# A Delta-rule stage moved from an automatic order into one explicit plan of all queues, with keys and queries no longer transposed on TensorE

## The chip, the cores and the metric

The kernel runs on one core of one Trainium2 chip. A core has TensorE (PE, whose weight loads are shown apart as PEld), VectorE (DVE), ScalarE (ACT), GpSimd (POOL) and SyncE (SP, used here only to issue DMAs). The metric is the device time of one launch in microseconds; lower is better.

## The reference

One decoder layer on a sequence of 1024 tokens, width 1024, float32. One normalised input feeds one projection; its columns go to two groups of heads that work in parallel:

```
h    = rms_norm(x, norm1_w);  proj = h @ w_in
A:   differential attention, 4 heads, two 64-wide softmax maps each
B:   gated DeltaNet, 4 heads of 128:
     qkv  = silu(causal_conv4(proj[...]))            # keys, queries, values
     q, k = l2_norm(q), l2_norm(k)
     L    = strict_lower(beta * k k^T * decay)       # per chunk of tokens
     u, w = solve(I + L, [beta v, beta k exp(g)])    # unit lower triangular
     state loop over chunks: v_new = u - w S;  o = q S + (q k^T * decay) v_new
                             S = S * exp(g_last) + k_dec^T v_new
x = x + concat(A, B) @ w_out
x = x + square(relu(rms_norm(x, norm2_w) @ w_up)) @ w_down
```

The chunk of the delta rule is free to choose as long as the result is the same; the kernel uses chunks of 128 tokens, eight for each head.

## The kernel before

**Arithmetic.** Large products are made as three float32r products of high and low parts (`hH`, `hL` for the input; `wH`, `wL` for weights). A weight piece comes from DRAM into `wraw`, ScalarE rounds it into `wH`, VectorE makes the rest `wL` (L303, L304; L1048, L1050 in the later part). Small products are plain float32.

**Order of the stages.** The normalised input and a first projection (`ps_z`, gates and decay inputs) come first, then the Delta stage, then the projections of group A (`da_units`, `ps_qk` and `ps_v`) overlapped with the scan of group B, attention, the output projection and the MLP.

**The Delta stage.** Six weight units are projected in the order keys, queries, values (`dn_proj(1)`, `dn_proj(0)`, `dn_proj(2)`), each unit two heads, each head two halves of 512 tokens: 24 tiles `ps_dn` of 24 products each, on TensorE at L309 to L311. A tile has the head's 128 channels on the partitions and 512 tokens (four chunks) along the row. Each tile is copied to `cp` (L761), convolved (one ScalarE operation, L763, and three VectorE operations, L765, into `cy`) and put through SiLU (L769 and L858 for keys, L773 else).

- Keys: the tile is parked in DRAM (L785), TensorE transposes it in four 128x128 pieces into `ps_t` (L813) and makes its Gram matrices `ps_m` (L820). ScalarE squares `ps_t` and accumulates each key's squared length (L865). From it VectorE makes the key scale `bp` = beta / length (L867 to L871) and the matrix `lt` = Gram * `bp` * decay (L877), and weights the transposed keys by `kds` (L882) for the scan. The diagonal 32x32 blocks of `lt` go to DRAM (`fsx_d`, L881). The decay matrices `dtm` come from rows loaded by GpSimd's queue (L830), two ScalarE operations (L834, L835) and a mask multiplied by GpSimd (L836).
- Queries: parked, transposed (L813) for their lengths (L938), multiplied with the reloaded keys (L820), scaled with `bp` and decay (L944), parked again. Between the tiles run the 31 steps of the blocks' inversion on VectorE (`invert`, L846 and L848).
- Values: turned by VectorE's 32x32 block transposition (L953) and stored with 128-byte runs (L791).
- The second half of the inverse (`horner`, L901 to L923) assembles the 128x128 inverses from the inverted blocks: products `ps_p` (L907) and three products `ps_h` (L915) a head, for two heads at a time, with VectorE and ScalarE between. Its result is `W`.

All of this stage was ordered by the framework's own scheduler.

**The explicit plan.** From `da_units` on, the class `Interleave` writes out by hand the order of every engine. Streams (`flow.add(priority, generator)`) emit TensorE work, tasks (`flow.task`) emit the operations of ScalarE (S), VectorE (V), GpSimd (G) and the DMA queues (P for SP, G for GpSimd). Each `yield` names an engine and a cost in ns, a time, or a condition. The plan keeps a clock for each engine, takes what can start first, and of several that are ready the one with the lower priority number, those ready for over 800 ns ahead of the others:

```
x = min(((r > s - SLACK, y.prio, y) for t, y, r in found
         if t <= s and isinstance(y.want, tuple) and y.want[0] == eng), key=lambda f: f[:2])[2]
```

A TensorE stream holds a PSUM bank (`flow.hold`) until a task leaves it. On the chip each engine runs its queue strictly in the written order. What the scheduler still orders (the last of the inverse's second half) falls between the written instructions; the plan allowed for it by a surcharge on the first products (`INVERSES`), and it started some steps at fixed times (`SCAN_START`, `NORM_START`, `EXP_AT`).

**The scan.** For each chunk c: products with the parked keys and the state (L1096), a remainder on VectorE (L1071), the product with `W` (L1105), a ScalarE copy `sy` (L1075), the product with the weighted keys (L1116), the update of the state on VectorE (L1084); beside it the outputs (L1148, L1164).

Of the kernel before, what the change touches and what calls it, by code (L numbers as in the profile page):

```python
# [18 lines left out]
P = 128  # L19
# [12 lines left out]
NORM_START = 12000.0  # L32
INVERSES = 650.0
BEGIN = -8400.0
BEFORE = dict(P=BEGIN + 2000.0)
SCAN_START = 29000.0
AHEAD = 3
EXP_AT = 16000.0
# [163 lines left out]
def act(n, accum=False):  # L202
    return "S", 55.0 + 0.83 * n + (280.0 if accum else 0.0)
# [23 lines left out]
def tile_hymba_layer(  # L227
# [54 lines left out]
    cg_d = dram.tile([32, P], F32, name="cg_d")  # L282
    qk_d = [dram.tile([P, SEQ], F32, name=f"qk_d{i}") for i in range(2 * HEADS)]
# [42 lines left out]
    make_identity(nc, ident)  # L326
    neghalf = const.tile([P, 32], F32, name="neghalf")
    V.memset(neghalf, -0.5)
    poshalf = const.tile([P, 4], F32, name="poshalf")
    V.memset(poshalf, 0.5)  # L330
# [22 lines left out]
    pj = pctx.enter_context(tc.tile_pool(name="pj", bufs=2, space=PSUM))  # L353
    p1ctx = ctx.enter_context(ExitStack())
    ph = p1ctx.enter_context(tc.tile_pool(name="ph", bufs=2, space=PSUM, side="right"))
# [360 lines left out]
    ps = ph.tile([P, 512], F32, tag="ph", name="ps_r")  # L716
    T.transpose(ps[0:32, 0:P], cg[:, 0:32], ident)
    V.tensor_copy(cgr, ps[0:32, 0:P])
    G.dma_start(cg_d, cgr)
# [6 lines left out]

    s1ctx = ExitStack()
    sf = s1ctx.enter_context(tc.tile_pool(name="sf", bufs=1, reuse_waits="tile", side="right"))
    sa = s1ctx.enter_context(tc.tile_pool(name="sa", bufs=1, reuse_waits="tile", side="right"))

    fx = sf.tile([P, 1024], F32, name="fx")
    fg = sf.tile([P, 1024], F32, name="fg")
    ft = sf.tile([P, 256], F32, name="ft")
    G.memset(fg, 0.0)
    G.memset(fg[:, ::33], 1.0)

    def ta(name, bufs, dt=F32):
        return sa.tile([P, 512], dt, tag=name, name=name, bufs=bufs)

    ssq, ssk, rq, bp, kds, vsc = smalls + [sp.tile([P, 32], F32, name=n) for n in ("kds", "vsc")]  # L740
    rvs = ssk

    cps = [sa.tile([P, 1028], F32, name=f"cp{i}") for i in range(2)]
    for cp in cps:
        V.memset(cp[:, 0:3], 0.0)

    copies = {}

    def dn_proj(kind):
        for pr in range(2):  # L750
            with tc.issue_after(x_last.ins) if kind == 1 and pr == 0 else ExitStack():
                w = load_unit(w_units[4 + 2 * kind + pr], behind=copies[1, 0, 0].ins if kind == 1 and pr == 1 else None)
            for hl in range(2):
                h = 2 * pr + hl
                u = 4 * kind + h
                cp = cps[hl]
                for hf in range(2):
                    ps = pj.tile([P, 512], F32, tag="pj", name="ps_dn")
                    trn(ps, w, hl * P, hf)
                    b = 512 * hf  # L760
                    copies[kind, h, hf] = S.copy(cp[:, 3 + b:3 + b + 512], ps)  # L761
                    y = ta("cy", 2)
                    S.activation(y, cp[:, 3 + b:3 + b + 512], AF.Copy, scale=pv[:, 36 + u:37 + u])  # L763
                    for wi in (2, 1, 0):
                        V.scalar_tensor_tensor(y, cp[:, wi + b:wi + b + 512], pv[:, 12 * wi + u:12 * wi + u + 1],  # L765
                                               y, ALU.mult, ALU.add)
                    if kind == 1:
                        th = ta("cth", 2)
                        S.activation(th, y, AF.Tanh, scale=0.5)  # L769
                        yield h, hf, y, th  # L770
                    else:
                        o = ta("cth" if hf else "k2", 2)
                        S.activation(o, y, AF.Silu)  # L773
                        yield h, hf, o

    def skew(gen):
        prev = None
        for it in gen:
            if prev is not None:
                yield prev  # L780
            prev = it
        yield prev

    def park(h, hf, slot, src):
        nc.sync.dma_start(park_d[h, 4 * hf:4 * hf + 4, :, slot, :].rearrange("c p d -> p c d"), v4(src))  # L785

    def put_blocks(dst, src):

        for a in range(4):
            s = slice(32 * a, 32 * a + 32)  # L790
            nc.sync.dma_start(dst[:, s].rearrange("(b s) r -> s b r", s=32),  # L791
                              src[s].rearrange("s (b r) -> s b r", r=32))

    def get_blocks(dst, src):

        k = dst.shape[1] // P
        src = src.rearrange("(a s) (k b r) -> b s k a r", s=32, k=k, r=32)
        for b in range(4):
            nc.sync.dma_start(dst[32 * b:32 * b + 32].rearrange("s (k a r) -> s k a r", k=k, r=32), src[b])
# [10 lines left out]
    def transposed(src):  # L810
        ps = pt_.tile([P, 512], F32, tag="pt", name="ps_t")
        for c in range(4):
            T.transpose(ps[:, c * P:(c + 1) * P], src[:, c * P:(c + 1) * P], ident)  # L813
        return ps

    def gram(l, r):
        ps = pm.tile([P, 512], F32, tag="pm", name="ps_m")
        for c in range(4):
            cs = slice(c * P, (c + 1) * P)
            T.matmul(ps[:, cs], l[:, cs], r[:, cs], start=True, stop=True)  # L820
        return ps

    dts = {}

    def decay(h, hf):
        if not dts:
            dts.update({(a, b): sa.tile([P, 512], F32, name=f"dtm{a}{b}") for a in range(HEADS) for b in range(2)})
        row = ta("row", 2)
        i = cidx(h, 4 * hf)
        G.dma_start(row, cg_d[i:i + 4, :].rearrange("i t -> (i t)").partition_broadcast(P))  # L830
        dtm = dts[h, hf]
        for c in range(4):
            cs = slice(c * P, (c + 1) * P)
            S.activation(dtm[:, cs], row[:, cs], AF.Relu, bias=cg[:, i + c:i + c + 1], scale=-1.0)  # L834
        S.activation(dtm, dtm, AF.Exp, scale=-1.0)  # L835
        G.tensor_tensor(v4(dtm), v4(dtm), bc_mask(tri), ALU.mult)  # L836

    def invert():

        fxv = fx.rearrange("p (j i) -> p j i", i=32)  # L840
        fgv = fg.rearrange("p (r c) -> p r c", c=32)
        nc.sync.dma_start(fx, fsx_d)
        for j in range(31):
            m = 31 - j
            tv = ft[:, :m * (j + 1)].rearrange("p (m c) -> p m c", m=m)
# [3 lines left out]
            if j % 8 == 7:  # L849
                yield  # L850
        nc.sync.dma_start(fsg_d, fg)

    lt = {}
    for h, hf, y, th in skew(dn_proj(1)):
        with tc.issue_after(copies[1, 0, 0].ins):
            decay(h, hf)
        k2 = ta("k2", 2)
        V.scalar_tensor_tensor(k2, th, 1.0, y, ALU.add, ALU.mult)  # L858
        park(h, hf, 0, k2)
        ps = transposed(k2)  # L860
        psm = gram(k2, k2)
        kn = ta("kn", 2)
        for c in range(4):
            i = cidx(h, 4 * hf + c)
            S.activation(kn[:, c * P:(c + 1) * P], ps[:, c * P:(c + 1) * P], AF.Square, accum_out=ssk[:, i:i + 1])  # L865
        sk = sp.tile([P, 4], F32, tag="sk", name="sk", bufs=2)
        V.tensor_scalar(sk, cols4(ssk, h, hf), 4.0 * EPS, None, ALU.add)  # L867
        r2 = sp.tile([P, 4], F32, tag="r2", name="r2", bufs=2)
        V.reciprocal(r2, sk)
        V.tensor_tensor(cols4(bp, h, hf), r2, cols4(beta, h, hf), ALU.mult)  # L870
        V.tensor_tensor(cols4(kds, h, hf), cols4(bp, h, hf), cols4(ediff, h, hf), ALU.mult)  # L871
        L = sp.tile([P, 512], F32, tag="lw", name="lt", bufs=10)
        lt[h, hf] = L
        for c in range(4):
            i = cidx(h, 4 * hf + c)
            cs = slice(c * P, (c + 1) * P)
            V.scalar_tensor_tensor(L[:, cs], psm[:, cs], bp[:, i:i + 1], dts[h, hf][:, cs], ALU.mult, ALU.mult)  # L877
        for b in range(4):
            bs = slice(32 * b, 32 * b + 32)
            p0 = 32 * h + 8 * b + 4 * hf  # L880
            nc.sync.dma_start(fsx_d[p0:p0 + 4, :].rearrange("c (j i) -> j c i", i=32), v4(L[bs, :])[:, :, bs])  # L881
# [65 lines left out]
    for _ in inverse:  # L947
        pass
# [1522 lines left out]
```

## Time and profile before

| | us |
|---|---|
| median of 3 runs | 1204.82 (1204.08 to 1206.37) |
| the profiled execution's own time | 1206.17 |
| its span, first to last instruction | 1204.5 |
| PE busy | 1188.2 |
| DVE busy | 853.3 |
| ACT busy | 610.9 |
| POOL busy | 152.2 |

The profiled execution's own time is 1.67 us more than its span, and 1.35 us above the median of the runs. In the profile's rows "idle before" is an engine's idle time just before an instruction, and the name behind the arrow is what ended it. The rows of a timeline give start, duration, engine, line, operation, the tiles written and read, and the count. TensorE is pipelined: durations of neighbouring matmuls overlap, and the distance of the starts is what one costs.

### The profile page before, as it was taken

What the parts mean: (1) busy time and instruction counts of PE and PEld (TensorE: products, weight loads), DVE (VectorE), ACT (ScalarE), POOL (GpSimd) and SP (SyncE); (2) the same over time, 40 slices, a digit from 0 to 9 for tenths busy, and PEclk for the clock granted to TensorE, in tenths of its full rate; (3) what the DMA queues carried; (4) which work ended last, traced back from release to release, by engine and by line L of the source; (5) the groups of instructions that cost most, each with busy time, mean ns of one, the idle gap of its engine ahead of it and who ended that gap; (6) DMA issues with size and microseconds to landing.
All of it is one profiled execution on the core that took longest, in us unless ns stands there. A gap on an engine that the chain in (4) does not pass through costs nothing.

```text
span 1204.5 us, 17444 instructions
## 1 busy us (share of the span) xinstructions
PE 1188.2 (99%) x6168; PEld 993.6 (82%) x6168; DVE 853.3 (71%) x1652; ACT 610.9 (51%) x1194; POOL 152.2 (13%) x191
## 2 busy tenths in 40 slices
PE   9999999999999999999999999999999999999998
PEld 8978888888887787888788888888888888888887
DVE  6869898647767889886895665456669755786543
ACT  6557553434546665774664544445553333333330
POOL 2425120023322432011100000000000000000000
PEclk9999999999999999999999999999999999999999
DMA  9345654565655586223546544344489455422401
GB/s 350 107 145 139 191 155 98 124 202 159 199 159 171 147 209 188 58 45 106 175 125 242 184 148 134 133 171 175 159 287 384 183 210 199 139 84 104 140 35 70
DMA packets 164494, 193.67 MB, mean 161 GB/s; under 512 B 63288, under 2 KB 119608, under 8 KB 164408
## 3 DMA queue, kind: packets, MB, share of 16 engines
q1 hardware_dynamic: 160136, 180.85, 47.2%
q0 software_dynamic: 4128, 11.72, 2.9%
q8 instruction: 48, 0.79, 0.3%
q14 instruction: 38, 0.31, 0.1%
q10 hardware_dynamic: 144, 0.00, 0.0%
HBM read 131.53 MB, written 61.00 MB: 160 GB/s over the span
## 4 chain that ended last, share of the span: by engine, by line
PE 83%; DVE 6%; DMA 4%; ACT 3%; issue 2%; POOL 1%; SPq 0%; POOLq 0%; DVEq 0%; ACTq 0%
PE X L2044 5%; PE X L2043 5%; PE X L2042 5%; PE X L2370 4%; PE X L2368 4%; PE X L2369 4%; PE ps_op L1829 2%; PE Y L2043 2%; PE Y L2042 2%; PE Y L2044 2%; PE ps_op L1831 2%; PE ps_op L1830 2%; PE ps_dn L311 2%; PE ps_dn L309 2%; PE Y L2368 2%
## 5 line engine op out<-in xcount | busy, mean ns | idle before, releaser
L1921 ACT CAST hH<-ur 128x1024 fp32r<-128x1024 f32 x56 | 58.8, 1050 | 173.3 <-PE Y L2369 89.4
L1922 DVE TENSOR_TENSOR hL<-ur,hH 128x1024 fp32r<-128x1024 f32 x56 | 68.4, 1223 | 79.5 <-ACT hH L1921 79.3
L1922 DVE TENSOR_TENSOR op<-raw,op 128x1024 fp32r<-128x1024 f32 x48 | 58.7, 1223 | 73.7 <-PE X L2043 40.4
L2370 PE MATMUL X<-hH,hL 128*128 128x512 f32 x224 | 87.2, 389 | 0.0
L2369 PE MATMUL X<-hL,hH 128*128 128x512 f32 x224 | 87.2, 389 | 0.0
L2368 PE MATMUL X<-hH 128*128 128x512 f32 x224 | 87.2, 389 | 0.0
L309 PE MATMUL ps_dn<-hH,wH 128*128 128x512 f32 x192 | 76.1, 396 | 1.8 <-ACT cp L761 1.8
L310 PE MATMUL ps_dn<-hL,wH 128*128 128x512 f32 x192 | 75.6, 394 | 0.0
L311 PE MATMUL ps_dn<-hH,wL 128*128 128x512 f32 x192 | 75.4, 393 | 0.0
L1922 DVE TENSOR_TENSOR hL<-dw,hH 128x1024 fp32r<-128x1024 f32 x56 | 68.2, 1219 | 1.0 <-ACT hH L1921 1.0
L1921 ACT CAST op<-raw 128x1024 fp32r<-128x1024 f32 x48 | 50.5, 1051 | 35.1 <-PE Y L2044 19.9
L1921 ACT CAST hH<-dw 128x1024 fp32r<-128x1024 f32 x56 | 58.6, 1046 | 10.8 <-DMA dw<-in_w_down_dram 5.1
L765 DVE SCALAR_TENSOR_TENSOR cy<-cp,pv,cy 128x512 f32<-128x512 f32 x72 | 57.2, 797 | 5.7 <-ACT cy L763 5.2
L1511 ACT ACTIVATE pexp<-pexp,mx,small 128x128 f32<-128x128 f32 (+7 forms) x64 | 55.2, 864 | 8.6 <-DVE mx L1531 8.3
L1829 PE MATMUL ps_op<-wH,hH 128*128 128x512 f32 x128 | 53.8, 420 | 0.9 <-DVE tq L1309 0.9
L1389 PE MATMUL ps_qk<-hH,wH 128*128 128x512 f32 x128 | 52.9, 413 | 0.0
L1391 PE MATMUL ps_qk<-hH,wL 128*128 128x512 f32 x128 | 50.6, 396 | 0.0
L1831 PE MATMUL ps_op<-wH,hL 128*128 128x512 f32 x128 | 50.2, 392 | 0.0
L1390 PE MATMUL ps_qk<-hL,wH 128*128 128x512 f32 x128 | 50.2, 392 | 0.0
L1830 PE MATMUL ps_op<-wL,hH 128*128 128x512 f32 x128 | 50.0, 391 | 0.0
L2042 PE MATMUL Y<-hH,op 128*128 128x512 f32 x128 | 49.8, 389 | 0.0
L2044 PE MATMUL Y<-hH,op 128*128 128x512 f32 x128 | 49.8, 389 | 0.0
(396 smaller groups left out, 3392.8 us busy)
## 6 DMA issues: line engine op xcount, KB each, us to landing
ur<-ud SPq DMA_DIRECT2D x28, 1024.0 KB, 4.8
raw<-in_w_up_dram SPq DMA_DIRECT2D x32, 512.0 KB, 4.0
dw<-in_w_down_dram SPq DMA_DIRECT2D x32, 512.0 KB, 6.6
wraw<-in_w_units_dram SPq DMA_DIRECT2D x40, 256.0 KB, 3.6
ud<-ua SPq DMA_DIRECT2D x16, 512.0 KB, 3.6
ud<-s SPq DMA_DIRECT2D x16, 512.0 KB, 2.6
pka<-park_d SPq DMA_DIRECT2D x32, 192.0 KB, 4.3
xt<-in_x_dram SPq DMA_DIRECT2D x8, 512.0 KB, 10.2
```

Source lines behind the costliest of these rows:

```text
L309: T.matmul(ps, lh(k), rh(k), start=(k == 0), stop=False)
L310: T.matmul(ps, lh(k), rl(k), start=False, stop=False)
L311: T.matmul(ps, ll(k), rh(k), start=False, stop=(k == n - 1))
L1829: T.matmul(ps, hH[:, kk, sl], wh[:, k, :], start=(k == 0), stop=False)
L1921: S.copy(dst[0], src)
L1922: V.tensor_tensor(dst[1], src, dst[0].bitcast(F32), ALU.subtract)
L2042: T.matmul(ps, op[0][:, k, cs], h[0][:, k, :], start=start and k == 0, stop=False, skip_group_check=True)
L2043: T.matmul(ps, op[0][:, k, cs], h[1][:, k, :], start=False, stop=False, skip_group_check=True)
L2044: T.matmul(ps, op[1][:, k, cs], h[0][:, k, :], start=False, stop=stop and k == 3, skip_group_check=True)
L2368: T.matmul(bank[t], v[0][:, j, sl], v[2][:, j], start=s0, stop=False, skip_group_check=True)
L2369: T.matmul(bank[t], v[0][:, j, sl], v[3][:, j], start=False, stop=False, skip_group_check=True)
L2370: T.matmul(bank[t], v[1][:, j, sl], v[2][:, j], start=False, stop=s1, skip_group_check=True)
```

## The change

It does four things.

1. The whole Delta stage becomes streams and tasks of the plan. `proj_units` runs the 24 Delta tiles (`dn_units`) and then the tiles of group A. `convolved` carries a tile from the bank to its SiLU; `grams`, `lower`, `crossed`, `inverted`, `side_work` (the decay rows, the sums of the queries, and the inverse's second half, each head's product issued on its own) and `weight_loads`/`weight_rounds` (priority 4) hold the rest. The plan starts at `BEGIN` = 57100 ns instead of inside the stage. `INVERSES` and the fixed starting times go. A task `opened` opens the memory of what follows once all tiles, Gram matrices and query sums are done and no Delta task is left; the first tile of group A and the scan wait for it. Scores and values wait until the inverse is complete.
2. Keys are no longer transposed on TensorE. VectorE turns them in 32x32 blocks (`token_major`) and they are stored, unweighted, with 128-byte runs as the values are. Their squared lengths are read from the diagonal of the unscaled Gram blocks.
3. The key scales move behind the inversion: `lower` multiplies the Gram matrix only with the decay (one 512-wide operation), the blocks are scaled by `bpx` in one 1024-wide operation after they were reloaded, and `lt` is scaled by 32 ScalarE operations (`columns`). `crossed` leaves the scale out of the query products too. In the scan the solved rows are scaled instead: `weighted` makes the operand of the state update on VectorE from the same PSUM bank that `solved` copies on ScalarE, and `solved` then scales its copy by four ScalarE operations, on which the second output product now waits.
4. Queries are no longer transposed on TensorE. ScalarE squares the tile, VectorE turns it in blocks and sums it (`squared`), one matmul with a selecting matrix adds the parts of all tiles, and the sums go through DRAM to their columns.

The core of the diff:

```diff
-BEGIN = -8400.0
-BEFORE = dict(P=BEGIN + 2000.0)
-SCAN_START = 29000.0
+BEGIN = 57100.0
+BEFORE = dict(S=BEGIN + 6500.0, V=BEGIN + 6500.0, P=BEGIN + 4000.0, G=BEGIN + 7000.0)
+SUMS_AT = BEGIN + 14000.0
...
-        ps = transposed(k2)
-        psm = gram(k2, k2)
-        for c in range(4):
-            S.activation(kn[:, ...], ps[:, ...], AF.Square, accum_out=ssk[:, i:i + 1])
-        ...
-        for c in range(4):
-            V.scalar_tensor_tensor(L[:, cs], psm[:, cs], bp[:, i:i + 1], dts[h, hf][:, cs], ALU.mult, ALU.mult)
-        V.tensor_tensor(v4(kn), v4(ps), bc_col(cols4(kds, h, hf)), ALU.mult)
-        park(h, hf, 1, kn)
...
+    def token_major(n, h, hf, slot, o):
+        V.transpose(t, o)
+        for a in range(4):
+            yield put(128, 512)
+            nc.sync.dma_start(dst[:, s].rearrange("(b s) r -> s b r", s=32), ...)
+    def squared(n, h, hf, o):
+        S.activation(sq, o, AF.Square)
+        V.transpose(t, sq)
+        V.tensor_reduce(part[:, m:m + 16], t.rearrange("p (b i) -> p b i", i=32), axis=AX.X, op=ALU.add)
+    def lower(n, h, hf, r, ps):
+        V.tensor_tensor(L, ps, dts[h, hf], ALU.mult)
+    def crossed(n, h, hf, r, ps):
+        V.tensor_tensor(qk, ps, dts[h, hf], ALU.mult)
+    def inverted():
+        yield when(lambda: state["fsx"] == 8)
+        nc.sync.dma_start(fx, fsx_d)
+        V.tensor_scalar(skx, fx[:, ::33], 4.0 * EPS, None, ALU.add)
+        V.reciprocal(rx, skx)
+        V.tensor_tensor(bpx, rx, betax, ALU.mult)
+        flow.task(2, columns(), "dn")
+        V.tensor_tensor(fxv, fxv, bpx.unsqueeze(2).broadcast_to([P, 32, 32]), ALU.mult)
+        ...

+    def columns():
+        G.tensor_tensor(vsc, sk, poshalf, ALU.pow)
+        for hf in range(2):
+            for h in range(HEADS):
+                for c in range(4):
+                    S.activation(x, x, AF.Copy, scale=bp[:, i:i + 1])
+    def opened():
+        yield when(lambda: state["dn"] and state["grams"] == 16 and state["rq"] and not flow.open["dn"])
+        s1ctx.close()
+        ...
+        state["open"] = True
+        yield when(lambda: state["horner"])
+        ...
+        state["px"] = True
...
-        def solved(y4):
-            S.copy(y4, psA)
+        def solved(c, y4, taken):
+            S.copy(y4, psA)
+            yield taken
+            for h in range(HEADS):
+                S.activation(part, part, AF.Copy, scale=bp[:, i:i + 1])
+        def weighted(c, w4):
+            V.tensor_tensor(v4(w4), v4(psA), bc_col(kds[:, c::8]), ALU.mult)
...
-            flow.pe(3 * n * fp32r(512) + (INVERSES if state["units"] < 4 else 0.0))
+            flow.pe(3 * n * fp32r(512))
...
+    flow.add(0.5, side_work())
+    flow.add(1, grams())
     flow.add(0, scan())
-    flow.add(3.5, values())
-    flow.add(3, scores())
-    flow.add(4, da_units())
+    flow.add(3.5, held_until("px", values))
+    flow.add(3, held_until("px", scores))
+    flow.add(4, proj_units())
+    flow.task(2, key_loads(), "dn")
+    flow.task(2, inverted(), "dn")
+    flow.task(1, opened())
```

More of the change, by code (lines that the diff above doesn't have):

```diff
@@ L725, in tile_hymba_layer @@
     n1ctx.close()
-    s1ctx = ExitStack()
[L728 to L733, printed above, removed]
+    ND = 6
+    DN_UNITS = [(kind, pr) for kind in (1, 0, 2) for pr in range(2)]
+    with tc.issue_after(x_last.ins):
+        first_unit = load_unit(w_units[6])
@@ L741, in tile_hymba_layer @@
-    rvs = ssk
-    cps = [sa.tile([P, 1028], F32, name=f"cp{i}") for i in range(2)]
+    G.memset(gb01, 0.0)
+    G.memset(gb23, 0.0)
+    cps = [sa.tile([P, 1028], F32, name=f"cp{i}") for i in range(4)]
+    dtms = [ah.tile([P, SEQ], F32, tag=f"KS{i}", name=f"dtm{i}") for i in range(2)]
+    dtms += [sa.tile([P, SEQ], F32, name=f"dtm{i}") for i in (2, 3)]
     for cp in cps:
         V.memset(cp[:, 0:3], 0.0)
[L747 to L774, printed above, removed]
@@ L808, in bc_mask, with take @@
         return t.unsqueeze(1).broadcast_to([P, 4, P])
-    def transposed(src):
-        ps = pt_.tile([P, 512], F32, tag="pt", name="ps_t")
-        for c in range(4):
[L813 to L817, printed above, removed]
+    flow = Interleave(BEGIN)
+    flow.free.update(BEFORE)
+    MK = 512 + P
+    used, users = {}, {}
+    def take(tag, n):
+        yield when(lambda: used.get(tag, 0) < n)
+        used[tag] = used.get(tag, 0) + 1
@@ L818, in gram, with decayed @@
+    def decayed(h, hf, row, at):
+        yield at
+        i = cidx(h, 4 * hf)
+        dt = dts[h, hf] = dtms[h][:, 512 * hf:512 * hf + 512]
         for c in range(4):
             cs = slice(c * P, (c + 1) * P)
[L820 to L831, printed above, removed]
-        for c in range(4):
[L833 to L836, printed above, removed]
@@ L848, in invert @@
             V.tensor_tensor(fgv[:, j + 1:32, 0:j + 1], fgv[:, j + 1:32, 0:j + 1], tv, ALU.subtract)
-            if j % 8 == 7:
-                yield
+        yield put(4096, P)
         nc.sync.dma_start(fsg_d, fg)
[L853 to L859, printed above, removed]
-        ps = transposed(k2)
-        psm = gram(k2, k2)
[L862 to L877, printed above, removed]
@@ L1056, in scan @@
         St, pks = {}, {}
+        yield when(lambda: state["open"] and state["W"] >= 4), None
         psA = pA.tile([P, 512], F32, name="ps_A")
@@ L1235, in exp_first @@
     def exp_first():
-        yield EXP_AT
+        yield when(lambda: state["open"])
         yield act(600)
```

551 lines of the change are left out of this document (405 added, 146 removed).

## The prediction

> **What bounds the kernel now.** I read the page first: one engine fills the span.
>
> ```profile
> span 1204.5 us, 17444 instructions
> PE 1188.2 (99%) x6168; PEld 993.6 (82%) x6168; DVE 853.3 (71%) x1652; ACT 610.9 (51%) x1194; POOL 152.2 (13%) x191
> ```
>
> TensorE (PE) is idle for 1204.5 - 1188.2 = 16.3 us in all. A gain must therefore be TensorE work taken away, or part of those 16.3 us. Next the busy times by stretch, for the Delta stage, which TensorE works on from 57 to 221 us. The columns are length, PE, PEld, DVE, ACT, POOL.
>
> ```profile
> 75.00:100.00 25.00, 23.16 (x120) 19.40 (x119) 19.24 (x40) 17.19 (x60) 11.68 (x13) 1.00 0.64 173
> 100.00:125.00 25.00, 23.05 (x122) 18.91 (x121) 24.05 (x43) 18.27 (x58) 10.56 (x9) 1.00 0.52 136
> 133.00:194.00 61.00, 61.00 (x317) 51.73 (x316) 55.89 (x153) 31.06 (x109) 10.17 (x9) 1.00 0.60 161
> sum 164.00, PE 160.12 PEld 133.72 DVE 135.67 ACT 91.88 POOL 39.40; mean PE 22.87 PEld 19.10 DVE 19.38 ACT 13.13 POOL 5.63
> ```
>
> The last row is the sum over 57 to 221 us: TensorE idles 164.00 - 160.12 = 3.9 us there, nearly all of it in the first two rows, the key part. In the query part (133 to 194 us) TensorE never idles, but VectorE is at 55.89 of 61 us: it is the next bound. The clock column is 1.00 throughout. The waits of TensorE from 45 to 400 us say what the idle time is:
>
> ```profile
> PE ps_dn L309 <- ACT cp L761: 1.8, 1, 1.8
> PE ps_at L1666 <- DVE pexp L1543: 1.8, 2, 1.5
> PE ps_t L813 <- DVE kn L882: 1.2, 1, 1.2
> PE ps_A L1105 <- DVE sr L1071: 0.8, 1, 0.8
> PE ps_t L813 <- DVE k L858: 0.8, 2, 0.6
> ```
>
> Three belong to the stage (1.8 + 1.2 + 0.8 = 3.8 us), and two of these three stand before a transposition (L813).
>
> **TensorE: what goes and comes.** The timeline shows what a transposition costs; the first and the last group of 16, and between them a return to the long products:
>
> ```profile
> 78.62 0.60 PE L813 MATMUL ps_t<-ident,k 128*128 128x128 f32 x4
> 79.05 1.06 PE L820 MATMUL ps_m<-k 128*128 128x128 f32 x8
> ...
> 87.10 0.48 PE L309 MATMUL ps_dn<-hH,wH 128*128 128x512 f32 x1
> 87.41 0.40 PE L310 MATMUL ps_dn<-hL,wH 128*128 128x512 f32 x1
> 87.65 0.40 PE L311 MATMUL ps_dn<-hH,wL 128*128 128x512 f32 x1
> ...
> 180.98 0.60 PE L813 MATMUL ps_t<-ident,cth 128*128 128x128 f32 x4
> 181.42 1.06 PE L820 MATMUL ps_m<-cth,kr 128*128 128x128 f32 x8
> 182.23 0.48 PE L311 MATMUL ps_dn<-hH,wL 128*128 128x512 f32 x1
> ```
>
> From start to start, four transpositions take 79.05 - 78.62 = 0.43 and 181.42 - 180.98 = 0.44 us. 16 groups by 0.435 us is **7.0 us that go**. The return to a 512-wide product costs a little more: 87.41 - 87.10 = 0.31 against 87.65 - 87.41 = 0.24 us; but the Gram products beside the transpositions stay, and so do their returns. The added matmul that sums the squared queries is a quarter of a Gram group (182.23 - 181.42 = 0.81 us), 0.2, and one return, 0.07: **+0.3 us**.
>
> [...]
>
> **VectorE, ScalarE, GpSimd.** Grouped by line, 50 to 330 us:
>
> ```profile
> L813 PE MATMUL ps_t<-ident,k 128*128 128x128 f32 x48 | 7.4, 277 | 2.0 <-DVE kn L882 1.2 <-DVE k L858 0.8
> L877 DVE SCALAR_TENSOR_TENSOR lt<-ps_m,small,dtm 128x128 f32<-128x128 f32 x32 | 8.9, 339 | 0.0
> L882 DVE TENSOR_TENSOR kn<-ps_t,kds 128x512 f32<-128x512 f32 x8 | 5.5, 685 | 0.1
> L944 DVE SCALAR_TENSOR_TENSOR qk<-ps_m,small,dtm 128x128 f32<-128x128 f32 x32 | 9.6, 342 | 0.0
> L871 DVE TENSOR_TENSOR kds<-small,ediff 128x4 f32<-128x4 f32 x8 | 2.4, 300 | 0.1
> L953 DVE STREAM_TRANSPOSE kn<-k 128x512 f32<-128x512 f32 x4 | 2.8, 700 | 0.4 <-ACT k L773 0.4
> L1315 DVE TENSOR_REDUCE part<-tq 128x16 f32<-128x512 f32 x8 | 5.5, 683 | 0.2
> L865 ACT ACTIVATE kn<-ps_t 128x128 f32<-128x128 f32 x32 | 8.3, 274 | 3.6 <-DVE cy L765 2.4 <-DMA park_d<-kn 1.2
> L865 ACT ACTIVATION_READ_ACCUMULATOR kn<-ps_t 128x1 f32 x32 | 6.6, 208 | 0.0
> L907 PE MATMUL ps_p<-gb,lt 128*128 128x96 f32 x64 | 7.8, 273 | 0.0
> L915 PE MATMUL ps_h<-W,pb 128*96 128x96 f32 (+2 forms) x192 | 14.2, 225 | 0.1
> ```
>
> A key tile loses four products from the Gram bank (L877, 8.9/8 = 1.1 us), the weighting (L882, 0.69) and four small column operations (L871 and its kind, by this row 2.4/8 = 0.3 each at most, 1.2); it gains one 512-wide product (as L882, 0.69) and one block transposition (L953, 0.70): about 1.6 us less, 13 us for eight tiles. A query tile loses four products (L944, 9.6/8 = 1.2); it gains a block transposition (0.70), a reduction (L1315, 0.68) and a 512-wide product (0.69): 0.87 more, 7.0 us for eight. The scaling of the 1024-wide inversion input adds two times L882, 1.4 us. VectorE has 4.6 us less in the stage, but 8.4 us more in the part where it was fullest. In the forecast this costs nothing: cover is the 61.00 - 55.89 = 5.1 us it had free there, and an inversion that can begin earlier, since the key part is 13 us lighter; that cover gone is the rival below.
>
> ScalarE loses the squares with accumulation (8.3 + 6.6 us for keys, as much for queries) and gains eight 512-wide squares and 64 scalings of 128 columns (half behind the inversion, half in the scan). At 0.3 us each, near the row of L865, that is about even; cover is its 13.13 busy of 23.4 us a stretch. GpSimd's sixteen powers of 4 columns become two of 32; all that GpSimd did in the query part was 10.17 us, which bounds one. What waits for them is the scale of the finished inverse and the closing of the stage; the query sums exist after the last query tile, eight value tiles (44 us) before the end: nothing.
>
> Stores: the weighted keys went out in 8 pieces; turned by VectorE they go out in 32, as the values do already (KB each, us to landing):
>
> ```profile
> park_d<-kn SPq DMA_DIRECT2D x32, 64.0 KB, 2.0
> ```
>
> 24 more issues on SP's queue, at 2.10 / 4 = 0.5 us each by the SP row below, are 12 us of SP in 164. They are first read by the scan; behind them on SP stand weight loads, gated a whole unit (22 us) ahead: nothing.
>
> **Waits.** The 1.2 and the 0.8 us go with the operation they stand before, and the keys' 0.8 us may only move to the Gram product, so I count 1.2 and half of 0.8, 1.6. Of the 1.8 us, where a copy stood behind decay work on ScalarE, the written-out order may remove all or none: between 0 and -1.8, I take -1.3, as the accumulating squares go from that same queue. **-2.9 us** (ends -3.8 and 0).
>
> **The seam behind the stage.** In the new plan the memory for what follows opens only when every Delta task has ended, stores included. Before, the tail looked so:
>
> ```profile
> 202.98 1.03 PE L907 MATMUL ps_p<-gb,lt 128*128 128x96 f32 x8
> 221.20 0.50 PE L1389 MATMUL ps_qk<-hH,wH 128*128 128x512 f32 x1
> 229.74 0.63 ACT L773 ACTIVATE cth<-cy 128x512 f32<-128x512 f32 x1
> 230.28 0.67 ACT L1303 ACTIVATE qk<-ps_qk,pv 128x512 f32<-128x512 f32 x1
> 232.34 2.10 SPq L791 DMA_DIRECT2D park_d<-kn  x4
> ```
>
> The last value tile's chain ended at 232.34 + 2.10 + 2.0 = 236.4, that is 15.2 us after TensorE went on. Two banks let TensorE run two tiles of 24 products ahead, 24 x 0.23 = 5.5 us each, 11 us; then two ScalarE operations of the first tile (0.67 each at most) and a transposition (0.70) must follow the opening, 2 us. 15.2 + 2 - 11 = 6.2 us of waiting, less what is left then of the inverse's second half, a pair of heads being (7.8 + 14.2) / 4 = 5.5 us of TensorE. With two pairs left nothing is lost, with none 6.2. Before, the first of it started only at 203 us, after the inversion, so I expect one or two left: **+1.5 us**.
>
> **Order.** Heads of a pair are now issued one by one: up to 16 more returns at 0.07 to 0.1, 0 to 1.6, taken **+0.8 us**. In the scan the state update waits for a weighting on VectorE (0.69) beside a copy on ScalarE, both from one bank:
>
> ```profile
> 321.57 0.58 ACT L1075 COPY sy<-ps_A 128x512 f32<-128x512 f32 x1 [1.73 <-PE ps_A L1105]
> 322.97 0.72 PE L1116 MATMUL ps_A<-sy,pka 128*128 128x128 f32 x5
> ```
>
> One behind the other costs 0.69 for each of 7 chunks, 4.8 us, if TensorE had no other work; it started 322.97 - 321.57 - 0.58 = 0.82 us after the copy anyway. 0 to 4.8, nearest to 0: **+0.5 us**.
>
> **Sum:** -7.0 + 0.3 - 2.9 + 1.5 + 0.8 + 0.5 = -6.8 us. Span 1204.5 - 6.8 = 1197.7; the profiled execution's own time 1206.17 becomes 1199.4; it stands 1.35 us above the median of the runs, 1204.82, from which I forecast **1198.0 us**. Behind the stage TensorE stays full, so I let the gain pass to the end undiminished.
>
> **Rivals.** (a) The seam costs its full 6.2 us because all of the inverse is done by then: 1198.0 - 1.5 + 6.2 = 1202.7. For it: an earlier inversion; against it: inversion steps share VectorE. (b) It ends slower: VectorE becomes the bound of the query part. There its load rises by 8.4 to 64.3 us, while TensorE brings the same tiles in 61.0 - 3.5 = 57.5 us. The parts of the weights that VectorE makes have the last priority in the plan of this stage, so TensorE then stands at a unit's first product. It decides from the point where less than 64.3 - 57.5 = 6.8 of the 13 us saved in the key part come forward, since the inversion can start only after the last key tile's pieces have landed. Price where nothing comes forward: the 6.8 us, and what the key part won, 3.5 of transpositions and 2.9 of waits, which has only turned into waiting: 1198.0 + 13.2 = 1211.2; with half of it 1204.6. For it: 55.89 of 61 us; against it: TensorE may run ahead by several tiles, and the value part after it is lighter on VectorE. [...] (c) All waits up to 400 us go, those of the first scores and the scan (1.8 + 0.8) too, and the seam costs nothing: 1204.82 - 7.0 + 0.3 - 3.8 - 2.6 = 1191.7.
>
> **Numbers.** Forecast 0.45 (1195 to 1201.5), (a) 0.20, (b) 0.20, (c) with the page's 0.02, 0.15. Between 1191 and 1208 lie the forecast, (a), most of (c) and the milder half of (b), about 0.8. A change under 0.2% (2.4 us) can't be told from none here. (a) lies across that bound, so faster 0.45 + 0.15 + 0.07, same 0.13, slower 0.20.
>
> **What would show it.** No transposition left in the stage; 512-wide products 0.23 us apart; the stage's TensorE idle time under 2 us; the first product after the stage near 212 to 216 us. Wrong if TensorE waits for a weight part (b), for the first tile's bank after the stage (a), or for the first product of the inverse's second half, which the order now fixes: a plan too fast for VectorE would show there.

## The result, and the profile after

| | before | after |
|---|---|---|
| median of 5 runs each, us | 1204.82 (1201.54 to 1206.90) | 1213.78 (1210.93 to 1214.99) |
| span of the profiled execution, us | 1204.5 | 1209.2 |
| PE busy, us | 1188.2 | 1187.8 |
| first product after the Delta stage, us | 221.20 | 208.13 |

The changed kernel is slower: 1.0071 times the time before, interval 1.0048 to 1.0094, where 1198.0 was forecast, in a range of 1191 to 1208. The profiled execution took 1210.93 us, the fastest of its five. TensorE leaves the Delta stage 13.07 us earlier, and yet the span is 4.7 us longer. So the part behind the stage takes 17.8 us more. First the engine totals of the page after, then the stretches (length, PE, PEld, DVE, ACT, POOL, granted clock, DMA share, GB/s): three that stood in the prediction, and the whole stage.

```profile
span 1209.2 us, 17215 instructions
PE 1187.8 (98%) x6106; PEld 990.8 (82%) x6106; DVE 854.0 (71%) x1600; ACT 617.3 (51%) x1138; POOL 142.4 (12%) x174
```

```profile
75.00:100.00 25.00, 25.00 (x127) 21.23 (x126) 21.48 (x29) 16.81 (x34) 5.70 (x6) 1.00 0.83 195
100.00:125.00 25.00, 23.91 (x116) 19.62 (x116) 20.95 (x24) 15.47 (x34) 7.70 (x8) 1.00 0.78 163
133.00:194.00 61.00, 59.28 (x292) 49.20 (x291) 59.60 (x126) 37.10 (x80) 10.20 (x2) 1.00 0.63 165
57.00:208.00 151.00, 148.15 (x714) 122.63 (x714) 131.87 (x253) 89.24 (x184) 32.18 (x25) 1.00 0.65 155
```

TensorE idles 151.00 - 148.15 = 2.85 us in the stage, and VectorE is at 59.60 of 61 us in the old query window. 62 products (6168 - 6106) are gone: 64 transpositions less, and two more for the one sum matmul, which stands as two in the trace (`ps_s` x2). TensorE's waits from 45 to 400 us, the view that was shown of before (here to 420), carry the result in their first line:

```profile
PE ps_o L1411 <- DVE oc L1400: 7.2, 2, 3.9
PE ps_m L921 <- DMA kr<-park_d: 1.2, 1, 1.2
PE ps_m L921 <- DVE k L829: 1.1, 2, 0.7
PE ps_A L1362 <- ACT sy L1305: 0.7, 1, 0.7
```

Twice, for 7.2 us in all, TensorE stands in the scan's second output product (`ps_o`, L1411) until VectorE has moved the first output product out of its bank (`decayed`, L1400). VectorE's own waits say what held it:

```profile
DVE oc L1400 <- DMA mixn_d<-oc: 10.6, 3, 5.2
```

The third of these waits, 1.1 us before chunk 5's eviction at 335.79, cost TensorE no stand.

The timeline around the first stand, TensorE, VectorE and GpSimd's queue:

```profile
343.20 1.05 PE L1394 MATMUL ps_o<-S,pkb 128*128 128x128 f32 x8
...
343.64 0.70 DVE L1443 STREAM_TRANSPOSE oc<-zgt 128x512 f32<-128x512 f32 x1
...
345.25 1.16 PE L1347 MATMUL ps_A<-sr,W 128*128 128x128 f32 x8
345.36 0.55 POOL L1446 DMA_DIRECT2D mixn_d<-oc  x1
...
349.57 0.69 DVE L1400 TENSOR_TENSOR oc<-ps_o,eg 128x512 f32<-128x512 f32 x1 [5.23 <-DMA mixn_d<-oc]
...
350.31 1.26 PE L1411 MATMUL ps_o<-sy,pkb 128*128 128x128 f32 x8 [3.90 <-DVE oc L1400]
```

The tiles `oc`, in which a chunk's output is put together, form a ring of two. Chunk 6 writes the tile that chunk 4 used. Chunk 6's first product is done at 344.25, but chunk 4's output was turned only by 344.34 and its store issued at 345.36; it landed 4.1 us later. The eviction stands in VectorE's queue until then, and the TensorE product behind it waits for the eviction. The plan that orders the queues knows VectorE, ScalarE and the banks; of this ring it knows nothing. Chunk 7 repeats it: its eviction starts at 370.61, after 4.3 us of waiting for chunk 5's store, and TensorE stands for 3.25 us.

In the kernel before, the plan knew as little of the same ring, but no eviction had to wait for it. Stores of `oc` and the evictions that come two chunks later, from its timeline, and the row of these stores among its DMA issues (count, KB each, us to landing):

```profile
350.44 0.55 POOL L1199 DMA_DIRECT2D mixn_d<-oc  x1 [4.23 <-DVE ri L1539]
...
359.93 0.69 DVE L1154 TENSOR_TENSOR oc<-ps_o,eg 128x512 f32<-128x512 f32 x1 [0.19 <-PE ps_o L1148]
...
366.21 0.60 POOL L1199 DMA_DIRECT2D mixn_d<-oc  x1 [0.63 <-DVE of L1709]
...
371.72 0.69 DVE L1154 TENSOR_TENSOR oc<-ps_o,eg 128x512 f32<-128x512 f32 x1
```

```profile
mixn_d<-oc POOLq DMA_DIRECT2D x8, 256.0 KB, 3.6
```

From issue to landing such a store takes 3.6 us in the median. The margin was 359.93 - 350.44 - 3.6 = 5.9 us for chunk 6 and 371.72 - 366.21 - 3.6 = 1.9 us for chunk 7 (1.4 us with the 4.1 that the store of the changed kernel took).

The stands cost more than their 7.2 us. Behind each, the granted clock (the third column from the right) falls; the stretches of 2 us around the first, and then two pairs of products from the timeline behind it:

```profile
348.00:350.00 2.00, 0.00 (x0) 0.00 (x0) 0.43 (x1) 0.54 (x2) 0.00 (x0) 1.00 0.38 141
350.00:352.00 2.00, 1.69 (x10) 1.59 (x11) 1.97 (x9) 0.00 (x0) 0.36 (x1) 0.81 0.07 12
352.00:354.00 2.00, 2.00 (x7) 1.52 (x6) 1.55 (x7) 0.41 (x1) 0.18 (x1) 0.50 0.75 221
354.00:356.00 2.00, 2.00 (x9) 1.42 (x9) 0.39 (x3) 1.65 (x5) 0.00 (x0) 0.84 0.00 0
```

```profile
351.80 0.63 PE L1613 MATMUL ps_v<-wL,hH 128*128 128x512 f32 x1
352.23 0.63 PE L1614 MATMUL ps_v<-wH,hL 128*128 128x512 f32 x1
...
354.72 0.39 PE L1614 MATMUL ps_v<-wH,hL 128*128 128x512 f32 x1
354.95 0.40 PE L1612 MATMUL ps_v<-wH,hH 128*128 128x512 f32 x1
```

From 351.23 to 354.72, eight 512-wide products take 3.49 us instead of 8 x 0.23 = 1.84 (0.23 from 354.72 to 354.95): 1.65 us lost. Behind the second stand the clock reads 0.93, 0.50 and 0.72 in the stretches from 370 to 376 us; 20 small products take 3.88 us there, where their like take about 2.2 (0.92 for the eight from 350.31, 1.04 for ten from 364.78), so 1.7 are lost. The two stands and their slow stretches are 7.15 + 3.4 = 10.6 us. The clock column gives the length of each slow stretch: (0.19 + 0.50 + 0.16) x 2 us = 1.7 us of clock are missing behind the first stand and (0.07 + 0.50 + 0.28) x 2 = 1.7 behind the second, that is 3.4 us at 0.50 each time. So in this trace stands of 3.90 and 3.25 us had 3.4 us at a clock of 0.50 behind each. Two of the runs below show about twice that, 6.8 and some 7 us.

### The profile page after: what moved, and what is told of

It is laid out like the page before. It is cut to its first block, busy times and chain, and to the rows that moved or that the text cites. A ratio compares the mean times of both kernels' runs of the same rounds, so it can differ in the third digit from the quotient of the medians.

```text
span 1209.2 us, 17215 instructions
## 1 busy us (share of the span) xinstructions
PE 1187.8 (98%) x6106; PEld 990.8 (82%) x6106; DVE 854.0 (71%) x1600; ACT 617.3 (51%) x1138; POOL 142.4 (12%) x174
## 4 chain that ended last, share of the span: by engine, by line
PE 82%; DVE 7%; DMA 5%; ACT 2%; issue 2%; SPq 1%; POOL 1%; POOLq 0%; DVEq 0%; ACTq 0%
PE X L2291 5%; PE X L2290 5%; PE X L2289 5%; PE X L2621 4%; PE X L2623 4%; PE X L2622 4%; PE Y L2290 2%; PE Y L2291 2%; PE ps_o L1933 2%; PE Y L2289 2%; PE Y L2621 2%; PE Z L2621 2%; PE Y L2622 2%; PE Z L2622 2%; PE Y L2623 2%
## 5 line engine op out<-in xcount | busy, mean ns | idle before, releaser
L1758 ACT ACTIVATE pexp<-pexp,mx,small 128x128 f32<-128x128 f32 (+7 forms) x64 | 55.1, 863 | 14.2 <-DVE mx L1778 13.9
L818 DVE SCALAR_TENSOR_TENSOR cy<-cp,pv,cy 128x512 f32<-128x512 f32 x72 | 53.4, 741 | 9.0 <-ACT cy L815 8.3
L1276 ACT CAST wH<-wraw 128x512 fp32r<-128x512 f32 x66 | 40.4, 616 | 28.5 <-PE ps_dn L1174 8.1
L1278 DVE TENSOR_TENSOR wL<-wraw,wH 128x512 fp32r<-128x512 f32 x60 | 43.9, 732 | 9.5 <-ACT wH L1276 9.4
## 6 DMA issues: line engine op xcount, KB each, us to landing
xt<-in_x_dram SPq DMA_DIRECT2D x8, 512.0 KB, 10.5
```

The lines of the kernel that those rows point to most:

```text
L1758: S.activation(e, e, AF.Exp, scale=negq[h][:, 8 * m + tb:8 * m + tb + 1], bias=bi[:, m:m + 1], accum_out=ssum[:, m:m + 1])
```

## The experiments

Theory A: the order puts a chunk's first output product too close to the store whose buffer it writes; the ring of two, unknown to the plan, is what costs. Theory B: the change made the way from the solved rows to the store longer on the chip (four ScalarE scalings a chunk), and the ring only shows it. Each ratio is to the kernel before on the same chip.

**Three tiles in the ring.**

```diff
-        oc = sb.tile([P, 512], F32, tag="oc", name="oc", bufs=2)
+        oc = sb.tile([P, 512], F32, tag="oc", name="oc", bufs=3)
-        ... tag="lw", bufs=10)      # and take("lw", 10)
+        ... tag="lw", bufs=9)       # makes the 2 KB of room
```

> Changed kernel with three output tiles oc in place of two; the 2 KB for it come from the ring lw, 9 tiles in place of 10. Theory A (the two oc tiles: a chunk's first output product is evicted into the tile that the chunk two before has not yet stored): the waits of VectorE for the store mixn_d, 10.6 us, and of TensorE behind it, 7.2 us, go, and so does the half clock after them (about 3.6 us): 1213.8 - 10.8 = 1203, from the profiled execution 1210.9 - 10.8 = 1200. Theory B (the outputs are late because the second output product waits for the four scalings of the solved rows on ScalarE): the third tile changes little, TensorE still waits 4 us or more in the scan, 1208 to 1214.

1201.35 us, ratio 0.9968 (0.9955 to 0.9980). No wait for the store is left; from 300 to 400 us TensorE is full at a granted clock of 1.00. These are its stretch there, its first wait from 240 us on, and chunk 4's store with chunk 6's eviction:

```profile
300.00:400.00 100.00, 99.79 (x626) 84.11 (x625) 72.95 (x252) 60.04 (x182) 31.84 (x42) 1.00 0.57 173
```

```profile
PE ps_A L1362 <- DVE sw L1316: 2.9, 2, 1.5
```

```profile
345.62 0.58 POOL L1446 DMA_DIRECT2D mixn_d<-oc  x1
345.88 0.69 DVE L1400 TENSOR_TENSOR oc<-ps_o,eg 128x512 f32<-128x512 f32 x1
```

The smaller ring `lw` changed the order a little too, but the order alone does not explain the gain: chunk 6's eviction starts 0.26 us after the issue of chunk 4's store, and chunk 7's 1.1 us after that of chunk 5's (361.57 and 360.45). With two tiles both would have had to wait for the landing; the third tile let them go. The span is 1198.7, 10.5 us under the changed kernel's, as the two stands and the slow clock add up to (10.6). By the ratios the gain is larger, 1.0071 - 0.9968 or about 12.4 us, as the changed kernel's profiled execution was its fastest. The third tile turns the change from a loss into a gain.

**The ring told to the plan** (two tiles, the next one begun only when the store is planned):

```diff
         yield loads, "pB"
+        if c > 1:
+            yield lambda: ends[c - 2].done, "pB"
```

> Changed kernel; the plan holds a chunk's output products back until the store of the chunk two before has landed in the plan. Buffers as they are. Theory A: TensorE does other products in that time instead of standing: the 7.2 us wait and the slow clock go, 1200 to 1203, unless the scan gets so late that the output projection waits for it (then 1203 to 1208). Theory B: outputs only get later, no gain, 1211 to 1216.

1202.86 us, ratio 0.9983 (0.9973 to 0.9993), no wait for the store. Another order, without a byte of memory, removes the stands as well.

**No scaling of the solved rows** (neither in the plan nor in the kernel; the second output product then uses unscaled rows):

```diff
-            yield taken
-            for h in range(HEADS):
-                yield act(P, False, 130.0)
-                S.activation(part, part, AF.Copy, scale=bp[:, i:i + 1])
```

> Changed kernel without the four scalings of the solved rows by bp on ScalarE (the outputs of group B lack that factor); the second output product waits for the copy alone, as before the change. Theory B: the waits in the scan go, 1200 to 1204. Theory A: outputs come some 1.5 us earlier a chunk, but the store still lands after the tile is wanted; at least one of the two waits stays, 1206 to 1213.

1203.67 us, ratio 0.9982 (0.9974 to 0.9991). The stands are nearly gone (VectorE waits 1.2 us for the store, TensorE 0.4), and the time lies where B expected it. But the plan drew up another order for the shorter queue, so this run doesn't separate the order from ScalarE's time.

**The same scalings planned, but not issued**, which keeps the order as it was:

```diff
                 yield act(P, False, 130.0)
-                S.activation(part, part, AF.Copy, scale=bp[:, i:i + 1])
+                pass
```

> The changed kernel in exactly its own order, but the four ScalarE scalings of the solved rows behind each chunk are not issued (the plan still counts them, the output lacks that scale). Theory A (the order puts a chunk's first output product too near to the store whose buffer it writes): the waits stay, TensorE idles 6 us or more for the eviction `decayed`, 1210 to 1215. Theory B (the scalings lengthen the way to the store): the stands shrink to under 2 us, 1200 to 1205.

1212.29 us, ratio 1.0067 (1.0054 to 1.0080). Its waits of TensorE and VectorE:

```profile
PE ps_o L1411 <- DVE oc L1400: 6.6, 2, 3.8
...
DVE oc L1400 <- DMA mixn_d<-oc: 9.6, 3, 5.2
```

ScalarE's time is not the cause: without it the stands are 6.6 us instead of 7.2. What the scalings did was to alter the plan. Theory B falls. Around the end of the first stand (3.8 us) the clock here reads 0.97 from 342 to 350 us, 0.50 to 354 and 0.71 to 358, by the count above 6.8 us at 0.50, of which TensorE worked some 5.5. Around that of the second (2.8 us) it reads 0.92 from 370 to 374 us and 0.65 to 378, 3.4 us at 0.50.

**The scan held back** to 265 us by a condition on time at its start (`yield BEGIN + 208000.0, None`):

> Changed kernel with the scan held until 265 us on the plan's clock, 11 us later than in the changed kernel and so near the kernel before, in which chunk 1 was solved at 281 and not at 266 us. Theory A: the tile is wanted 11 us later while the end of each output stays where the shared engines put it: the waits for mixn_d go, 1200 to 1204. Theory B: the chain of a chunk is as long as it was, the waits move along, 1210 to 1215.

1216.04 us, ratio 1.0087 (1.0072 to 1.0101), above both ranges and nearest to B's. The edit moved the scan further than meant: chunk 1's solved rows are copied at 295.87, where the changed kernel has 267.56 and the kernel before 282.33. The stands stay all the same (7.9 us, three of them, the longest 5.0; from 350 to 400 us the clock reads 0.93, so 3.5 us of clock are missing there, some 7 us at 0.50). My addition to A, that the scan comes too early, was wrong. That leaves, of theory A, the distance within the scan between one chunk's store and the next but one chunk's first product.

**The stand filled with work.** For chunks 6 and 7 the first output product is made four times over:

```diff
-            for h in range(HEADS):
-                T.matmul(o1[...], pkb[h][:, 0, :], Sold[h], start=True, stop=True)
+            for again in range(4 if c > 5 else 1):
+                for h in range(HEADS):
+                    T.matmul(o1[...], pkb[h][:, 0, :], Sold[h], start=True, stop=True)
```

> The changed kernel with the first output product of chunks 6 and 7 made four times over instead of once (same values, same order otherwise): about 3 us more TensorE work just ahead of each of the two stands, so that TensorE stands about 1 us instead of 3.9 and 3.25. If the clock falls because TensorE stands, the clock stays at 1.00 from 350 to 358 and from 370 to 378 us, and although 6 us of useless products are added the time falls by the cost of the slow clock, about 3.5 us: near 1209.5 to 1211.5. If the fall has another cause, or the buffer is what costs and not the stand, the clock stays at 0.65 to 0.92 there and the time is that of the changed kernel, 1213 to 1215, or above.

1208.99 us, ratio 1.0037 (1.0023 to 1.0051), just under the range expected. VectorE still waits 9.3 us for the store, TensorE stands 0.8 us instead of 7.2, and the clock does not fall, here or behind the second place:

```profile
350.00:352.00 2.00, 1.63 (x15) 1.25 (x14) 0.82 (x3) 0.44 (x1) 0.00 (x0) 1.00 0.34 123
352.00:354.00 2.00, 2.00 (x13) 1.83 (x14) 2.00 (x9) 1.62 (x6) 0.54 (x1) 1.00 0.49 141
```

The added products take 2 x 2.7 = 5.4 us of TensorE by the distance of starts (0.89 us for one making, from 363.89 to 364.78 in the changed kernel), and yet the ratio falls from 1.0071 to 1.0037, about 4 us, with intervals that just touch. The stands are 6.4 us shorter and the products take 5.4, so about 3 us remain for the slow clock, near the 3.4 us of the trace. The clock column itself shows that it was the standing that lowered the clock here: the same order, with VectorE's waits of 9.3 us instead of 10.6, but with TensorE standing 0.8 us instead of 7.2, keeps 1.00 from 342 to 378 us.

**Ring of three and told to the plan** (the condition with `ends[c - 3]`):

> The changed kernel with three tiles in the ring of outputs and the plan told of the ring (chunk c begins its output only when the end of chunk c - 3 is done). With three tiles alone the ring no longer bound anywhere, so the condition should change little: 1200 to 1203, within 0.2% of three tiles alone; no wait for the store of the outputs, granted clock 1.00 from 300 to 400 us. A rival: the condition reorders the plan and the waits of the state update (2.9 us with three tiles alone) move: down to 1198.5 or up to 1205.

1201.25 us, ratio 0.9972 (0.9963 to 0.9980): the same as three tiles alone. The wait for the state update's operand is 1.9 us instead of 2.9. Both versions beat the kernel before.

**The kernel before without its transpositions** (lengths and weighted keys are then made from the tile that wasn't turned):

```diff
-        ps = transposed(k2)      # and transposed(q2)
+        ps = k2                  # and q2
```

> The kernel before, with only the 64 transpositions of keys and queries on TensorE left out: what read ps_t reads the tile itself instead (so the lengths and the weighted keys are computed from other values). Everything else, the accumulating squares and the 32 Gram products with their scales, stays. The prediction's term: 16 groups by 0.435 us, 7.0 us of TensorE, and the waits 1.2 and half of 0.8 before them: 1204.8 - 8.6 = about 1196.2, range 1194.5 to 1199. [...] If TensorE's time in the stage were hidden behind VectorE: 1203 to 1205.

1200.21 us, ratio 0.9964 (0.9951 to 0.9977), that is 4.3 us less, above the range expected and half of the 8.6 us. Its profiled span is 1198.9, 5.6 us less, though the stage began 1.5 us later there (58.67 against 57.13). The stage itself is 155.47 us instead of 164.07; 1.5 us of the difference is work of the inverse that came behind it. Its waits of TensorE inside the stage:

```profile
PE ps_p L907 <- DMA gb<-fsg_d: 0.9, 1, 0.9
PE ps_dn L309 <- ACT cp L761: 0.8, 1, 0.8
PE ps_m L820 <- ACT k L773: 0.8, 1, 0.8
PE ps_m L820 <- DVE k L858: 0.6, 1, 0.6
PE ps_m L820 <- ACT kn L938: 0.4, 1, 0.4
```

The 7.0 us of transpositions go, but the waits do not: they now stand before the Gram product (0.8 + 0.6 + 0.4 us), and 0.9 us came up before the inverse. The ratio is that of the changed kernel with three tiles (0.9968), within the intervals: nothing shows that the rest of the change gained time beyond the transpositions. This kernel makes other values, though, and leaves out work that a valid one must do elsewhere.

**The kernel before with its store doubled, and fourfold** (the same store of `oc` issued two or four times):

> The kernel before, with the store of each finished output chunk issued twice, so that its buffer comes free later. In its own trace the last eviction of a first output product (371.72 us) starts 1.4 us after the landing of the store whose buffer it writes (366.21 + 4.1). If the ring is the cause of the loss and the kernel before only just escapes it, a second store (0.6 us to issue and up to 4 to land) brings a wait of VectorE for the store at this place, with TensorE standing up to 2 us and no more than that: 1203 to 1209. If the ring does not matter for the kernel before: no wait for the store, and the time of the kernel before, 1203.5 to 1205.5.

1208.38 us, ratio 1.0038 (1.0023 to 1.0053). In its timeline and its waits the stand appears at the place named, chunk 7's eviction:

```profile
378.16 0.69 DVE L1154 TENSOR_TENSOR oc<-ps_o,eg 128x512 f32<-128x512 f32 x1 [0.96 <-DMA mixn_d<-oc]
```

```profile
PE ps_o L1164 <- DVE oc L1154: 2.3, 1, 2.3
```

The second store was issued 4.5 us after the first (369.42 and 373.89), as GpSimd's queue held it until the first had landed (3.88 us idle before it, ended by that landing), and VectorE then waited 0.96 us for the buffer; the margin in this run was thus some 3.5 us, near the 1.9 read from the kernel before. Of the 2.3 us stand only these 0.96 are the ring's: before them VectorE was still at other work, part of which had waited for GpSimd. The rest of the 4.6 us by which the kernel is slower lies outside the ring, for example in waits for the remainder (1.9 us, before 0.8) and for a weight part (1.5, before none). So the run shows that the kernel before was a few microseconds from this wait, and not what the ring costs. The stand left the clock at 1.00.

> The same with four stores each, about 2 us more of issue and up to three landings more. If the ring is the cause: VectorE waits for the store several times, TensorE stands for 3 us or more at least once, the granted clock falls behind that stand as in the changed kernel, and the time rises by 4 to 15 us: 1208 to 1220. If not: the time of the kernel before plus what the further traffic costs, 1203.5 to 1206.

1258.03 us, ratio 1.0451 (1.0426 to 1.0477), far above both expectations. Each further store was issued only after the one before it had landed (28.5, 25.0 and 17.4 us of GpSimd's queue before the second, third and fourth issue of the eight chunks), and what stands behind them in that queue is late too: VectorE waits 33.5 us for GpSimd's `of` of group A, with two stores 9.4. VectorE's wait for the buffer is only 1.9 us, once. The dose hit the queue, not the ring, and says nothing about the theory.

## Why the prediction was wrong

Its account of the transpositions held; a sentence after the sum failed, and three terms had the wrong size. From the distances of TensorE's starts, between the stage's first projection product (57.13, 57.08 and 58.67 us) and the first product behind the stage (221.20, 208.13 and 214.14), a wait counted with the product before it:

| us of TensorE | before | after | before, no transpositions |
|---|---|---|---|
| projection tiles (576 products), waits included | 138.31 | 136.84 | 137.46 |
| Gram products (128), waits included | 13.55 | 13.29 | 14.35 |
| transpositions (64) | 7.07 | none | none |
| the sum matmul | none | 0.34 | none |
| second half of the inverse | 4.56 | none | 3.08 |
| stage | 164.07 | 151.05 | 155.47 |

(Gate and decay products, 0.58 us, are left out of the rows.) The last row but one is not a gain: this work only moved behind the stage.

- Transpositions, -7.0: right, 7.07. No run shows the price that the 0.02 beside (c) stood for: by their mean duration, 277 ns, 64 would be 17.7 us, and in the kernel before without its transpositions the stage fell by 8.6 us, 1.5 of it moved work. Starts, not durations, set the price here.
- Sum matmul, +0.3: right, 0.34.
- Waits of the stage, -2.9: too large. TensorE's idle time there fell from 3.9 to 2.85, so -1.0, and not under the 2 us named; the waits moved on to the Gram product (L921: 1.2 for reloaded keys, 1.1 for the keys). The step "the 1.2 and the 0.8 us go with the operation they stand before" failed; the kernel with nothing but the transpositions taken out shows it.
- Seam, +1.5: nothing. The whole inverse was left behind the stage, the case "with two pairs left nothing is lost", and TensorE began with 36 products of group A without a gap. Rival (a) didn't come. A pair of heads costs 4.6 us there by the starts, not the 5.5 that were added up from durations. For the same reason the first product came at 208.13, ahead of the 212 to 216 named.
- VectorE, rival (b): VectorE filled up in the query window (59.60 of 61 us) as its working said, but no product waited for a weight part.
- Order of the heads, +0.8: too small. In the stage, projections and Gram products together took 1.7 us less, 1.0 of it waits. But the inverse's second half, whose heads are issued one by one, now ran wholly behind the stage, and over both places its products took 21.95 us from start to start against 19.75 before: 19 returns to the long products instead of 15, and 1.6 us of waits for its own operands, where the kernel before has none and the sum had no term:

```profile
PE ps_h L1146 <- DVE pb L1075: 0.7, 2, 0.4
PE ps_h L1146 <- ACT W L1085: 0.6, 1, 0.6
PE ps_h L1146 <- DVE W L1082: 0.3, 1, 0.3
```

- Scan operand, +0.5: too small. The two readers of the bank went one behind the other in all seven chunks, as feared; before the state update TensorE waited 0.7 us in the changed kernel, 3.3 us with three tiles in the ring (2.9 of it in two chunks where VectorE came to the weighting late), 2.3 with three and the plan; the kernel before had none there.

With the ring out of the way the span is 1198.7, against the 1197.7 of the sum. That nearness is in part luck. The terms above missed in both directions, the waits of the first scores (1.8 us before, 0.2 with three tiles) went without having been counted, and by the ratio 0.9968 the gain is 3.9 us where 6.8 were forecast. What the sum had no term for at all is the 10.6 us of the outputs' buffer. Of the 17.8 us behind the stage they are the greater part; the inverse, of which 15.2 us stood there before and 21.95 do now, is 6.8 more. The sentence that failed is "Behind the stage TensorE stays full, so I let the gain pass to the end undiminished". It took the scan as it was, though the whole plan behind the stage was to be drawn up anew, and looked at one operand of it. All rivals lay in the stage, its seam or the state update. Rows of before could have given the missing one: a margin of 1.9 us between a landing store and the next writer of its tile, in an order that the plan did not tie to that landing. Its price could have been bounded too, by one landing a chunk.

Why the new order lost those 1.9 us and more is known only in part. It isn't ScalarE's scaling time and not the scan's start; the order with the scalings planned brings the stands, the one without hardly any. The traces narrow it down: from the addition of a chunk's second output product to the turning of its output, VectorE's starts lie 8.7, 13.9 and 14.9 us apart for chunks 3, 4 and 5 in the kernel before, and 17.9, 15.4 and 27.9 in the changed one (the last with the first stand in it). So the new order finishes these outputs later. Which choice of the plan decides that was not traced.

## What to carry to other kernels

When a change makes a planner draw its order up anew, list every buffer ring that the plan does not model, and read from the trace before how long after its last reader's landing each tile is written again; a margin of 2 us in a kernel with 4 us stores is a rival with a price. Tell the planner of the ring, or give it one tile more. Price a TensorE stand as long as those here (2.8 to 5.0 us) with its slow clock, in the changed kernel half as much again (3.4 us for 7.15).

## What was not expected of the hardware

- Stands of 3.25 and 3.90 us were followed by a clock of 0.50 for 3.4 us, one of 2.8 us (scalings not issued) goes with 3.4 us too, one of 3.8 us (the same run) with 6.8, and where the scan is held back (longest stand 5.0 us) some 7 us are at 0.50 from 350 to 400 us; stands of 1.5 us (three tiles) and 2.3 us (store doubled) were followed by none. With the scan held back the clock also reads 0.97 from 250 to 300 us, where TensorE's longest wait is 2.4 us and its idle time 3.5 us in all. Useless work, put into the stand, kept the clock at 1.00 and cost less than it saved (ratio 1.0037 against 1.0071).
- VectorE and ScalarE reading the same bank did not overlap in any of the seven chunks of the changed kernel, whichever went first; one pair:

```profile
334.03 0.69 DVE L1316 TENSOR_TENSOR sw<-ps_A,kds 128x512 f32<-128x512 f32 x1 [1.86 <-PE ps_A L1347]
334.75 0.59 ACT L1305 COPY sy<-ps_A 128x512 f32<-128x512 f32 x1 [5.47 <-DVE sw L1316]
```

  The second starts 0.03 us after the first's end, and the row names VectorE as what released it, so the program made it wait. Whether the chip would let them overlap without that wait was not tried.
